# A decoder trunk on one core: the opening, GpSimd's work of the first stage and the weight of the output norm are arranged in another way

## The chip, the cores and the metric

The kernel runs as one program on one core of a Trainium2 chip. The core has TensorE (PE, with its weight loads as PEld), VectorE (DVE), ScalarE (ACT), GpSimd (POOL) and SyncE (SP, which issues DMAs), each with an instruction stream of its own; they meet by semaphores. SBUF holds the tiles, PSUM what TensorE writes. The metric is the time of one execution in microseconds (us) on the device; lower is better.

## The reference

Two layers work on 256 tokens of width 1024. Each mixes the tokens, cross-attends into 256 memory tokens, and applies an MLP. Only the first mixer is touched:

```python
z = rmsnorm(x, g) @ w_in
u, q, k, v, gate, beta_l, alpha_l = split_cols(z, A_SIZES)   # 512 x 5, 4, 4
y_pool = multiscale_pool(u, pool_w, pool_scale)
y_dn = gated_deltanet(q, k, v, gate, beta_l, alpha_l, ...)
x = x + concatenate([y_pool, y_dn]) @ w_out
```

The delta net (4 heads of 128) takes q, k and v through a short causal convolution and silu, and builds in each chunk of 64 tokens a lower triangular matrix from k k^T, beta and the decay. It solves `(I + a_low) T = I`, scans over the chunks, and ends with `rmsnorm(o, o_norm) * silu(gate)`, where `o_norm` holds one weight for each of a head's 128 channels.

## The kernel before

Every large matmul is done three times with float32 split into a high and a low part (`mm3`, L195 to L197: hi by hi, lo by hi, hi by lo). A weight tile comes by DMA on SP into one of four `raw` buffers; ScalarE makes `hi` from it (L185), VectorE, now and then GpSimd, the rest `lo` (L186). An activation that leaves PSUM is split likewise by `evac_hl` into `hh` (ScalarE, L243) and `hl` (VectorE, L247). PSUM has three pools: four `acc`, two `mb`, two `tp`.

After 13 warm-up matmuls (L145) the first mixer, `mixer0`, opens in an order written by hand for ScalarE, VectorE and TensorE. It norms x (sums of squares of token block 0 on ScalarE, `bn_stats` of block 1 on VectorE, the power -0.5 on GpSimd, L277), writes the two scales into diagonal matrices `dr` (L393), and transposes and scales x at once with real matmuls x·diag (L401). With the transposed x it computes the `a_ba` projection (beta, alpha and half of the gate) and two blocks of `a_k`. `conv_silu` does the convolution (`ct`, L416 to L421; its output `cv`, L426).

From there the order of the steps is the list `MIX`: `g1` the other half of the gate, `kn0`, `kn1` the transposes of k to tokens (L515) with their sums of squares and the copy into `pk`, `cum` the decay, `q0` to `q3`, `v0` to `v3`, `u0` to `u3` projection blocks, `kr` the norms of k (`sA`, `sK`, `sV`), `e0`, `e1` the decay matrices (`kk`, `am`, L547; mask `et`, L545), `i0`, `i1` the start of the inverse of 32x32 blocks (`ec`, the masked copies `al`, `T`, its transpose `bc`, L580 to L591), `inv1` to `inv6` its steps (L574), `mem` and `k0` to `k8` the memory tokens' norm, transposes (`memT`, L325) and keys, `pk` the scaling of `pk` (L560), `qn`, `vn`, `t1` to `t4` the scan and its outputs, `po0` to `po3` the pooling. A scheduler then places the instructions of each engine; the DMA of a weight starts when a `raw` buffer comes free. GpSimd multiplies the gate by half the output weight (`GO`, `onh`, L453).

Of the kernel before, what the change touches and what calls it, by code (L numbers as in the profile page):

```python
# [67 lines left out]
def trunk(ctx: ExitStack, tc: tile.TileContext, A, out, upto=99):  # L68
# [308 lines left out]
    def mixer0():  # L377
        hT = []
        dr = [gt('ct', 4)[:, :P] for _ in range(2)]

        def norm():

            r, s2, bn, mv = (small([P, w], f"n0_{i}", 1) for i, w in enumerate((2, 2, 12, 2)))
            for n in range(2):
                sumsq(xs[0][n], s2[:, n:n + 1])
                dve.bn_stats(bn[:, 6 * n:6 * n + 6], xs[1][n])
            dve.tensor_add(r[:, 0:1], s2[:, 0:1], s2[:, 1:2])
            rsqrt_into(r[:, 0:1], r[:, 0:1], EPS, D)
            dve.bn_aggr(mv, bn)
            dve.scalar_tensor_tensor(r[:, 1:2], mv[:, 0:1], mv[:, 0:1], mv[:, 1:2], op0=ALU.mult, op1=ALU.add)  # L390
            rsqrt_into(r[:, 1:2], r[:, 1:2], EPS, 1)
            for t in range(2):
                dve.tensor_scalar(dr[t], ident, r[:, t:t + 1], None, op0=ALU.mult)  # L393

        def tokens(n):

            ps = [tp() for _ in range(2)]
            for i in range(2):
                for j in range(2):
                    for t in range(2):  # L400
                        pe.matmul(ps[i][:, j * S + t * P:j * S + (t + 1) * P], x_block(t, 4 * n + 2 * i + j), dr[t], start=True, stop=True)  # L401
            new = [hpair() for _ in range(4)]

            for k in (0, 2, 1, 3):
                evac_hl(ps[k // 2][:, (k % 2) * S:(k % 2 + 1) * S], new[k], V("a_ln")[:, 4 * n + k:4 * n + k + 1])
            hT.extend(new)
# [42 lines left out]
        def ev_gate(t, q, ps):  # L449
            if t == 0:  # L450
                dve.tensor_scalar(onh, V("o_norm"), 0.5, None, op0=ALU.mult)
            gate_half(t, ps, S)
            pool.tensor_tensor(b3(GO[t], P), b3(GO[t], P), onh.unsqueeze(1).to_broadcast([P, 4, P]), op=ALU.mult)  # L453

        with tc.manual_schedule(engines={mybir.EngineType.Activation, mybir.EngineType.DVE, mybir.EngineType.PE}):
            norm()
            tokens(0)
            us = list(wunit("a_ba", 0, 1056))
            tokens(1)
            us += wunit("a_ba", 1, 1056)  # L460
# [944 lines left out]
```

## Time and profile before

| | us |
|---|---|
| median of 3 runs (873.1 to 874.53) | 874.26 |
| the profiled execution's own time | 871.83 |
| its span in the trace | 870.0 |
| TensorE busy | 848.6 (98%) |
| VectorE busy | 541.3 (62%) |
| ScalarE busy | 492.8 (57%) |
| GpSimd busy | 214.4 (25%) |

The profile takes one execution. Its span is the time from the first to the last recorded event. A timeline row gives start and duration in us, the engine, the line of the kernel, the operation, output<-input, the shapes and a count; in brackets how long the engine had been idle before and who released it. Windows give each engine's busy time in a stretch, with the clock that was granted to TensorE (1.00 is 2.4 GHz) and the share of the DMA engines' time.

### The profile page before, as it was taken

What the parts mean: (1) busy time and instruction counts of PE and PEld (TensorE: products, weight loads), DVE (VectorE), ACT (ScalarE), POOL (GpSimd) and SP (SyncE); (2) the same over time, 40 slices, a digit from 0 to 9 for tenths busy, and PEclk for the clock granted to TensorE, in tenths of its full rate; (3) what the DMA queues carried; (4) which work ended last, traced back from release to release, by engine and by line L of the source; (5) the groups of instructions that cost most, each with busy time, mean ns of one, the idle gap of its engine ahead of it and who ended that gap; (6) DMA issues with size and microseconds to landing.
All of it is one profiled execution on the core that took longest, in us unless ns stands there. A gap on an engine that the chain in (4) does not pass through costs nothing.

```text
span 870.0 us, 16157 instructions
## 1 busy us (share of the span) xinstructions
PE 848.6 (98%) x6247; PEld 769.0 (88%) x6247; DVE 541.3 (62%) x1050; ACT 492.8 (57%) x996; POOL 214.4 (25%) x195
## 2 busy tenths in 40 slices
PE   7889999999999999999999999999999999999996
PEld 5888999899889999999889888888998999999995
DVE  5988756656566555555557697865565755555554
ACT  5774556655565554454576767856554655544552
POOL 1142520310013222222233454544200122222220
PEclk9999999999999999999999999999999999999999
DMA  7632443666446566656654421135644466566641
GB/s 263 222 97 84 132 140 113 178 197 194 160 135 212 184 184 190 192 187 184 218 156 160 147 81 66 50 116 160 185 147 146 150 212 189 181 188 193 192 147 49
DMA packets 41261, 138.84 MB, mean 160 GB/s; under 512 B 4576, under 2 KB 5088, under 8 KB 41184
## 3 DMA queue, kind: packets, MB, share of 16 engines
q1 hardware_dynamic: 40320, 136.28, 50.2%
q10 hardware_dynamic: 864, 1.52, 0.5%
q8 instruction: 49, 0.80, 0.4%
q14 instruction: 28, 0.23, 0.1%
HBM read 136.74 MB, written 1.05 MB: 158 GB/s over the span
## 4 chain that ended last, share of the span: by engine, by line
PE 89%; DVE 4%; ACT 1%; issue 0%; POOL 0%; POOLq 0%; ACTq 0%; DVEq 0%
PE acc L197 12%; PE acc L195 12%; PE acc L196 12%; PE mb L196 10%; PE mb L195 10%; PE mb L197 10%; PE tp L195 4%; PE tp L196 4%; PE tp L197 4%; PE acc L574 1%; PE tp L257 1%; PE tp L1222 1%; DVE ct L419 1%; PE tp L1225 1%; DVE lo L186 1%; PE tp L1205 0%
## 5 line engine op out<-in xcount | busy, mean ns | idle before, releaser
L185 ACT ACTIVATE hi<-raw 128x1024 fp32r<-128x1024 f32 (+2 forms) x256 | 264.1, 1034 | 260.5 <-PE acc L197 117.5
L186 DVE TENSOR_TENSOR lo<-raw,hi 128x1024 fp32r<-128x1024 f32 (+3 forms) x227 | 277.4, 1224 | 197.6 <-ACT hi L185 196.9
L197 PE MATMUL acc<-hi,hl 128*128 128x512 f32 (+3 forms) x496 | 188.5, 380 | 0.0
L196 PE MATMUL acc<-lo,hh 128*128 128x512 f32 (+3 forms) x496 | 188.4, 380 | 0.0
L195 PE MATMUL acc<-hi,hh 128*128 128x512 f32 (+3 forms) x496 | 188.2, 379 | 0.0
L195 PE MATMUL mb<-hh,hi 128*128 128x256 f32 x640 | 182.7, 287 | 0.5 <-ACT ct L417 0.5
L196 PE MATMUL mb<-hl,hi 128*128 128x256 f32 x640 | 182.3, 286 | 0.0
L197 PE MATMUL mb<-hh,lo 128*128 128x256 f32 x640 | 180.5, 283 | 0.0
L924 POOL TENSOR_TENSOR rs<-rs 128x256 f32<-128x256 f32 x64 | 74.6, 1175 | 238.3 <-ACT rs L922 238.3
L196 PEld LDWEIGHTS mb<-hl,hi 128*128 128x128 f32 x640 | 122.0, 191 | 2.2 <-issue 1.0
L195 PEld LDWEIGHTS mb<-hh,hi 128*128 128x128 f32 x640 | 121.9, 191 | 1.9 <-ACT ct L417 0.7
L197 PEld LDWEIGHTS mb<-hh,lo 128*128 128x128 f32 x640 | 121.9, 191 | 0.0
L197 PEld LDWEIGHTS acc<-hi,hl 128*128 128x128 f32 x496 | 93.3, 188 | 17.6 <-DVE hl L245 0.3
L196 PEld LDWEIGHTS acc<-lo,hh 128*128 128x128 f32 x496 | 93.5, 188 | 17.2
L195 PEld LDWEIGHTS acc<-hi,hh 128*128 128x128 f32 x496 | 93.3, 188 | 17.3
L186 POOL TENSOR_TENSOR lo<-raw,hi 128x1024 fp32r<-128x1024 f32 (+2 forms) x29 | 68.7, 2369 | 92.6 <-ACT hi L185 85.9
L195 PE MATMUL tp<-hh,hi 128*128 128x256 f32 x256 | 72.1, 282 | 0.0
L196 PE MATMUL tp<-hl,hi 128*128 128x256 f32 x256 | 71.9, 281 | 0.0
L197 PE MATMUL tp<-hh,lo 128*128 128x256 f32 x256 | 71.7, 280 | 0.0
L197 PEld LDWEIGHTS tp<-hh,lo 128*128 128x128 f32 x256 | 48.4, 189 | 0.0
L196 PEld LDWEIGHTS tp<-hl,hi 128*128 128x128 f32 x256 | 48.2, 188 | 0.0
L195 PEld LDWEIGHTS tp<-hh,hi 128*128 128x128 f32 x256 | 48.2, 188 | 0.0
(304 smaller groups left out, 1257.5 us busy)
## 6 DMA issues: line engine op xcount, KB each, us to landing
raw<-in_ff_w_dram SPq DMA_DIRECT2D x128, 512.0 KB, 3.6
raw<-in_xa_wk_dram SPq DMA_DIRECT2D x16, 512.0 KB, 4.0
raw<-in_xa_wv_dram SPq DMA_DIRECT2D x16, 512.0 KB, 3.8
raw<-in_xa_wq_dram SPq DMA_DIRECT2D x16, 512.0 KB, 3.9
raw<-in_xa_wo_dram SPq DMA_DIRECT2D x16, 512.0 KB, 3.5
raw<-in_a_w_out_dram SPq DMA_DIRECT2D x8, 512.0 KB, 3.5
raw<-in_c_q_dram SPq DMA_DIRECT2D x8, 512.0 KB, 4.2
raw<-in_c_w_out_dram SPq DMA_DIRECT2D x8, 512.0 KB, 3.2
```

The lines of the kernel that those rows point to most:

```text
L185: act.activation(hi[:, :n], raw[:, :n], AF.Copy)
L186: lo_eng.tensor_sub(lo[:, :n], raw[:, :n], f(hi[:, :n]))
L195: pe.matmul(ps, sh, mh, start=start, stop=False)
L196: pe.matmul(ps, sh, ml, start=False, stop=False)
L197: pe.matmul(ps, sl, mh, start=False, stop=stop)
L257: pe.transpose(ps[:, j * S + t * P:j * S + (t + 1) * P], src(t, k0 + j), ident)
L419: dve.scalar_tensor_tensor(c[:, 3 - j:], xp[:, :S - 3 + j], w[:, j:j + 1], c[:, 3 - j:], op0=ALU.mult, op1=ALU.add)
L574: pe.matmul(ps[o, c], lhs[o, c], rhs[o, c], start=True, stop=True)
L924: pool.tensor_tensor(sq, rl, rl, op=ALU.mult)
L1222: pe.matmul(po[rows, :S], v, pts[a][bi][:, :S], start=bi == 0, stop=False)
L1225: pe.matmul(po[:, :S], CV[g][:64], pcT[:64], start=False, stop=True)
```

## The change

The opening scales x itself by the norm into four tiles `xn` (VectorE the first half of the columns, ScalarE the second) and transposes them with plain `pe.transpose`. The sum of squares of a token block's first half is ScalarE's, that of its second half VectorE's (`tensor_tensor_reduce`). The second halves of x are loaded on ScalarE's DMA queue; two `a_ba` tiles share a `raw` buffer. `onh` shrinks to one number for each channel and is applied as the scale when the transposed output leaves PSUM in `out_t`, where GpSimd's multiply of the gate is dropped. The first copies `ec` of the inverse, `pk_scale` and the copies to `memT` go to ScalarE, the wide mask product `al` to VectorE; the `et` masks become steps of their own late in the list, and GpSimd too now follows the list. The list has another order.

```diff
-MIX = """g1 kn0 kn1 cum q0 q1 kr e0 i0 e1 v0 q2 v1 i1 inv1 v2 q3 inv2 mem v3 inv3 vn0 inv4 k0 inv5 u0
-u1 u2 pk u3 k1 k2 qn0 pw qn1 po0 inv6 po1 vn1 po2 k3 k4 t1 k5 k6 t2 po3 t3 k7 k8 t4 sh0""".split()
+MIX = """g1 kn1 q0 kn0 cum q1 kr e1 e0 v0 i0 q2 i1 inv1 v1 v2 q3 inv2 inv3 mem v3 k0 inv4 vn0 inv5 u0 et1 u1 u2 pk u3 et0 k1 k2 pw qn0 qn1
+po0 inv6 po1 vn1 po2 k3 k4 t1 k5 k6 t2 po3 t3 k7 k8 t4 sh0""".split()
...
-    ("w2_k", P), ("w2_v", 64), ("o_norm", P),
+    ("w2_k", P), ("w2_v", 64), ("o_norm", 1),
...
+        raw = wraw.tile([P, 1056], F32, tag="raw", name=nm("raw"))
+        for j in range(2):
+            first[name, i + j] = raw[:, j * n:(j + 1) * n]
+            nc.sync.dma_start(first[name, i + j], A[name][i + j])
+    for t in range(2):
+        nc.sync.dma_start(xs[t][0], A["x"][t, 0])
+        nc.scalar.dma_start(xs[t][1], A["x"][t, 1])
+    nc.sync.dma_start(cst[:, :P], A["cst"][:, :P])
+    early("a_ba", 0, 528)
     nc.sync.dma_start(vec, A["vec"])
-    for i in range(4):
-        early("a_ba", i, 528)
+    early("a_ba", 2, 528)
     nc.sync.dma_start(cst[:, P:], A["cst"][:, P:])
...
-                dve.tensor_copy(memT[:, k0:k0 + 2, :], b3(ps, S))
+                act.activation(memT[:, k0:k0 + 2, :], b3(ps, S), AF.Copy)
...
+        hT = [None] * KT
+        xn = [[gt('cv', 6) for _ in range(2)] for _ in range(2)]
+        n_r, n_s, n_q = (small([P, 2], f"n0_{i}", 1) for i in range(3))
+        def norm_act(t):
+            act.activation(junk, xs[t][0], AF.Square, scale=D ** -0.5, accum_out=n_s[:, t:t + 1])
+        def norm_dve(t):
+            dve.tensor_tensor_reduce(out=xn[t][1], in0=xs[t][1], in1=xs[t][1], scale=1.0 / D, scalar=EPS,
+                                     op0=ALU.mult, op1=ALU.add, accum_out=n_q[:, t:t + 1])
+        def norm_pow(t):
+            r = n_r[:, t:t + 1]
+            dve.tensor_add(r, n_s[:, t:t + 1], n_q[:, t:t + 1])
+            pool.tensor_tensor(r, r, mhalf[:, :1], op=ALU.pow)
+        def norm_mul(t):
+            r = n_r[:, t:t + 1]
+            dve.tensor_scalar(xn[t][0], xs[t][0], r, None, op0=ALU.mult)
+            act.activation(xn[t][1], xs[t][1], AF.Copy, scale=r)
+        def evac_x(ps, k):
+            hT[k] = hpair()
+            evac_hl(ps[k // 2][:, (k % 2) * S:(k % 2 + 1) * S], hT[k], V("a_ln")[:, k:k + 1])
...
-        onh = gt('onh', 1, P)
+        onh = small([P, 1], "onh", 1)
...
-            if t == 0:
-                dve.tensor_scalar(onh, V("o_norm"), 0.5, None, op0=ALU.mult)
             gate_half(t, ps, S)
-            pool.tensor_tensor(b3(GO[t], P), b3(GO[t], P), onh.unsqueeze(1).to_broadcast([P, 4, P]), op=ALU.mult)
...
+            pt = [tp(), tp(), acc(), acc()]
+            def flip(t):
+                for k in range(KT):
+                    pe.transpose(pt[k // 2][:, (k % 2) * S + t * P:(k % 2) * S + (t + 1) * P], xn[t][k // 4][:, (k % 4) * P:(k % 4 + 1) * P], ident)
+            norm_act(0)
+            norm_dve(0)
+            norm_pow(0)
+            norm_act(1)
+            norm_mul(0)
+            norm_dve(1)
+            flip(0)
+            norm_pow(1)
+            us = [wsplit("a_ba", 0, 528)]
+            norm_mul(1)
+            flip(1)
+            us.append(wsplit("a_ba", 1, 528))
             ps = [acc() for _ in range(2)]
-            for j, (hi, lo) in enumerate(us):
-                h3, l3 = b3(hi[:, :528], 264), b3(lo[:, :528], 264)
-                for t in range(2):
-                    for k2 in range(2):
-                        k = 2 * j + k2
+            def first_mm(j):
+                for k2 in range(2):
+                    k = 2 * j + k2
+                    h3, l3 = (b3(z[:, :528], 264) for z in us[j])
+                    for t in range(2):
                         mm3(ps[t][:, :264], tuple(a[:, t * P:(t + 1) * P] for a in hT[k]), (h3[:, k2], l3[:, k2]), k == 0, k == KT - 1)
+            for j in range(4):
+                for k in (2 * j, 2 * j + 1):
+                    evac_x(pt, k)
+                if j < 2:
+                    us.append(wsplit("a_ba", j + 2, 528))
+                first_mm(j)
...
+        dve.tensor_scalar(onh, V("o_norm"), 0.5, None, op0=ALU.mult)
...
-            e_, et, am = gt('e', 2), gt('et', 2), gt('am', 2)
+            e_, am = gt('et', 2), gt('am', 2)
...
-            pool.tensor_tensor(b3(et, P), b3(e_, P), U.unsqueeze(1).to_broadcast([P, 4, P]), op=ALU.mult)
...
+        def e_mask(t):
+            pool.tensor_tensor(b3(AT[t], P), b3(AT[t], P), U.unsqueeze(1).to_broadcast([P, 4, P]), op=ALU.mult)
         def pk_scale():
             for t, w in ((0, ela), (1, sK)):
-                pool.tensor_tensor(b3(pk[t], P), b3(pk[t], P), w[:, t].unsqueeze(2).to_broadcast([P, 4, P]), op=ALU.mult)
+                for h in range(4):
+                    act.activation(pk[t][:, hs(h)], pk[t][:, hs(h)], AF.Copy, scale=w[:, t, h:h + 1])
...
-                (dve if t == 0 else pool).tensor_copy(b3(ec, 32)[o], b3(E[t], P)[o, :, o])
+                act.activation(b3(ec, 32)[o], b3(E[t], P)[o, :, o], AF.Copy)
             am = gt('al', 2, 5 * P)
             a4 = am.rearrange("p (l h j) -> p l h j", l=5, h=4)
             m3 = b3(C("masks"), 32)
-            for l0, l1 in ((0, 1), (1, 5)):
+            def part(l0, l1):
                 n = l1 - l0
-                (pool if l0 else dve).tensor_tensor(a4[:, l0:l1], b3(ec, 32).unsqueeze(1).to_broadcast([P, n, 4, 32]),
-                                                    m3[:, l0:l1].unsqueeze(2).to_broadcast([P, n, 4, 32]), op=ALU.mult)
+                dve.tensor_tensor(a4[:, l0:l1], b3(ec, 32).unsqueeze(1).to_broadcast([P, n, 4, 32]),
+                                  m3[:, l0:l1].unsqueeze(2).to_broadcast([P, n, 4, 32]), op=ALU.mult)
+            part(0, 1)
             T_ = gt('T', 2)
             dve.tensor_tensor(b3(T_[:, :P], 32), C("ident32").unsqueeze(1).to_broadcast([P, 4, 32]), a4[:, 0], op=ALU.subtract)
             B_ = gt('bc', 2, P)
             dve.transpose(B_, T_[:, :P])
+            part(1, 5)
...
-                evac_hl(ps[:, hs(h)], (hi[:, t * P:(t + 1) * P], lo[:, t * P:(t + 1) * P]))
+                evac_hl(ps[:, hs(h)], (hi[:, t * P:(t + 1) * P], lo[:, t * P:(t + 1) * P]), onh)
...
-        run(MIX, step)
+        with tc.manual_schedule(engines={mybir.EngineType.Pool}):
+            run(MIX, step)
...
-    put("o_norm", g["a_o_norm"][0][None])
+    put("o_norm", g["a_o_norm"][0][:, None])
```

VectorE at the opening, before: `n` are the small tiles of the norm, `onh` the output weight, `ct` the diagonal matrices.

```order
L386 BN_STATS n_2_14_135<-x_84 128x6
L386 BN_STATS n_2_14_135<-x_85 128x6
L387 TENSOR_TENSOR n_0_12_133<-n_1_13_134 128x1
L451 TENSOR_SCALAR onh_127<-vec 128x128
L276 TENSOR_SCALAR n_0_12_133<-n_0_12_133 128x1
L389 BN_AGGR n_3_15_136<-n_2_14_135 128x2
L390 SCALAR_TENSOR_TENSOR n_0_12_133<-n_3_15_136 128x1
L276 TENSOR_SCALAR n_0_12_133<-n_0_12_133 128x1
L393 TENSOR_SCALAR ct_125<-cst,n_0_12_133 128x128
L393 TENSOR_SCALAR ct_126<-cst,n_0_12_133 128x128
```

VectorE at the opening now (ISA is the multiply-and-sum and its read-out, `cv_123` to `cv_126` the scaled x, `raw_93` and `raw_97` the a_ba tiles):

```order
L389 ISA cv_124,n_2_10_129<-x_83 128x512
L389 ISA n_2_10_129 128x1
L394 TENSOR_TENSOR n_0_8_127<-n_1_9_128,n_2_10_129 128x1
L494 TENSOR_SCALAR onh_130<-vec 128x1
L399 TENSOR_SCALAR cv_123<-x_82,n_0_8_127 128x512
L389 ISA cv_126,n_2_10_129<-x_85 128x512
L389 ISA n_2_10_129 128x1
L394 TENSOR_TENSOR n_0_8_127<-n_1_9_128,n_2_10_129 128x1
L188 TENSOR_TENSOR lo_159<-raw_93,hi_158 128x528
L399 TENSOR_SCALAR cv_125<-x_84,n_0_8_127 128x512
L188 TENSOR_TENSOR lo_173<-raw_93,hi_172 128x528
L249 SCALAR_TENSOR_TENSOR hl_179<-tp_136,vec,hh_178 128x256
```

`onh`, which reads `vec`, stands before the first scaling of x, and the statistics of the second block behind it.

ScalarE at the opening now; `x_83` and `x_85` are the second halves of x:

```order
L493 ACTIVATE ea_360<-vec 128x4
L400 ACTIVATE cv_124<-x_83,n_0_8_127 128x512
L187 ACTIVATE hi_158<-raw_93 128x528
L400 ACTIVATE cv_126<-x_85,n_0_8_127 128x512
L187 ACTIVATE hi_172<-raw_93 128x528
L245 ACTIVATE hh_178<-tp_136,vec 128x256
L245 ACTIVATE hh_182<-tp_136,vec 128x256
L187 ACTIVATE hi_186<-raw_97 128x528
L245 ACTIVATE hh_202<-tp_137,vec 128x256
L245 ACTIVATE hh_206<-tp_137,vec 128x256
L187 ACTIVATE hi_210<-raw_97 128x528
L187 ACTIVATE hi_277<-raw_275 128x1024
```

`ea`, which reads `vec`, stands ahead of the scaling; all hi of a_ba and the first of a_k stand ahead of the last four `hh`, which follow after two more a_k tiles.

VectorE at the start of the inverse, before:

```order
L186 TENSOR_TENSOR lo_973<-raw_970,hi_972 128x1024
L547 SCALAR_TENSOR_TENSOR am_675<-acc_668,sA_464,e_673 128x128 x4
L547 SCALAR_TENSOR_TENSOR am_710<-acc_703,sA_464,e_708 128x128
L580 COPY ec_686<-am_675 32x128 x4
L547 SCALAR_TENSOR_TENSOR am_710<-acc_703,sA_464,e_708 128x128
L586 TENSOR_TENSOR al_691<-ec_686,cst 128x128
L547 SCALAR_TENSOR_TENSOR am_710<-acc_703,sA_464,e_708 128x128
L589 TENSOR_TENSOR T_694<-cst,al_691 128x128
L547 SCALAR_TENSOR_TENSOR am_710<-acc_703,sA_464,e_708 128x128
L591 STREAM_TRANSPOSE bc_696<-T_694 128x128
```

VectorE there now (the e matrix of the second block comes first):

```order
L561 SCALAR_TENSOR_TENSOR am_693<-acc_687,sA_463,et_692 128x128 x4
L417 SCALAR_TENSOR_TENSOR ct_734<-ct_734,vec 128x254
L417 SCALAR_TENSOR_TENSOR ct_786<-ct_786,vec 128x255
L417 SCALAR_TENSOR_TENSOR ct_734<-ct_734,vec 128x253
L605 TENSOR_TENSOR al_748<-ec_743,cst 128x128
L605 TENSOR_TENSOR al_748<-ec_743,cst 128x512
L609 TENSOR_TENSOR T_750<-cst,al_748 128x128
L424 SCALAR_TENSOR_TENSOR cv_741<-ct_734 128x256
L611 STREAM_TRANSPOSE bc_752<-T_750 128x128
L417 SCALAR_TENSOR_TENSOR ct_786<-ct_786,vec 128x254
L605 TENSOR_TENSOR al_800<-ec_795,cst 128x128
L417 SCALAR_TENSOR_TENSOR ct_786<-ct_786,vec 128x253
```

The `ec` copies are gone from VectorE, and both wide `al` masks (128x512) stand in it.

ScalarE there now:

```order
L559 ACTIVATE et_692<-et_692 128x512
L414 ACTIVATE ct_786<-mb_761 128x256
L415 ACTIVATE ct_786<-mb_761,vec 128x256
L273 ACTIVATE junk,ss_1167<-mem_1162 128x512
L187 ACTIVATE hi_1434<-raw_1432 128x1024
L598 ACTIVATE ec_743<-am_693 32x128 x4
L414 ACTIVATE ct_916<-mb_891 128x256
L415 ACTIVATE ct_916<-mb_891,vec 128x256
L419 ACTIVATE ct_734<-ct_734 128x256
L598 ACTIVATE ec_795<-am_672 32x128 x4
L187 ACTIVATE hi_1477<-raw_1475 128x1024
```

The two groups of four `ec` copies stand behind a `hi` and the convolutions' copies of two blocks. Between the matmuls of `kk` and the first of `inv1`, TensorE has 90 projection matmuls now and had 72.

## Rows read from the trace of the kernel before

**Rows 1.** The page: busy time, share and instructions of each engine.
```profile
PE 848.6 (98%) x6247; PEld 769.0 (88%) x6247; DVE 541.3 (62%) x1050; ACT 492.8 (57%) x996; POOL 214.4 (25%) x195
```

**Rows 2.** TensorE's waits: line, releaser: us in total, times, longest.
```profile
PE tp L401 <- DVE ct L393: 3.4, 1, 3.4
...
PE acc L574 <- DVE bc L591: 2.6, 1, 2.6
...
PE acc L574 <- DVE rstd L285: 0.9, 1, 0.9
```

**Rows 3.** Windows: from:to, length, busy PE, PEld, DVE, ACT, POOL, clock, DMA, GB/s.
```profile
5.50:9.00 3.50, 0.14 (x2) 0.06 (x1) 1.73 (x8) 0.93 (x3) 0.98 (x2) 1.00 1.04 388
...
40.00:70.00 30.00, 24.75 (x210) 24.33 (x209) 26.66 (x51) 19.30 (x53) 16.39 (x14) 0.89 0.37 116
45.00:50.00 5.00, 5.00 (x33) 5.00 (x31) 2.28 (x4) 3.79 (x17) 0.00 (x0) 0.66 0.65 202
50.00:60.00 10.00, 10.00 (x88) 10.00 (x88) 9.44 (x25) 9.91 (x26) 6.24 (x5) 1.00 0.16 39
...
70.00:90.00 20.00, 19.09 (x461) 17.55 (x460) 16.71 (x43) 10.47 (x26) 2.35 (x2) 1.00 0.27 82
```

**Rows 4.** Timeline of the opening, to the first a_k evacuation.
```profile
6.92 0.69 DVE L386 BATCH_NORM_STATS2 n<-x 128x6 f32<-128x512 f32 x1 [2.08 <-DMA x<-in_x_dram]
7.55 0.20 ACT L479 ACTIVATE ea<-vec 128x4 f32<-128x4 f32 x1 [0.54 <-DMA vec<-in_vec_dram]
8.02 1.08 POOL L277 TENSOR_TENSOR n<-n,mhalf 128x1 f32<-128x1 f32 x2 [6.27 <-DVE n L389]
8.95 2.35 PE L401 MATMUL tp<-ct,x 128*128 128x128 f32 x16 [3.36 <-DVE ct L393]
...
11.33 0.84 ACT L243 ACTIVATE hh<-tp,vec 128x256 fp32r<-128x256 f32 x2 [0.42 <-PE tp L401]
12.73 1.17 ACT L185 ACTIVATE hi<-raw 128x528 fp32r<-128x528 f32 x2
17.68 1.06 ACT L185 ACTIVATE hi<-raw 128x1024 fp32r<-128x1024 f32 x1 [0.23 <-DMA raw<-in_a_k_dram]
...
26.95 0.39 PE L195 MATMUL mb<-hh,hi 128*128 128x256 f32 x1 [0.51 <-ACT ct L417]
```

**Rows 5.** Timeline from 36 to 70 us, around the two stalls.
```profile
36.00 1.22 DVE L186 TENSOR_TENSOR lo<-raw,hi 128x1024 fp32r<-128x1024 f32 x1
...
40.15 3.50 POOL L453 TENSOR_TENSOR GO<-GO,onh 128x512 f32<-128x512 f32 x2 [31.00 <-DVE GO L443]
40.32 2.21 DVE L186 TENSOR_TENSOR lo<-raw,hi 128x1024 fp32r<-128x1024 f32 x1
42.45 1.48 DVE L426 SCALAR_TENSOR_TENSOR cv<-ct 128x256 f32<-128x256 f32 x1
43.98 0.44 PE L515 MATMUL tp<-cst,cv 128*128 128x128 f32 x2 [2.66 <-DVE cv L426]
...
55.56 1.26 DVE L527 TENSOR_TENSOR sK<-sA,egc 128x8 f32<-128x8 f32 x1
59.17 2.95 DVE L580 COPY ec<-am 32x128 f32<-32x128 f32 x4
62.42 1.20 DVE L586 TENSOR_TENSOR al<-ec,cst 128x128 f32<-128x128 f32 x1
64.70 0.87 PE L574 MATMUL acc<-bc,al 32*32 32x32 f32 x32 [2.60 <-DVE bc L591]
68.79 0.28 DVE L586 TENSOR_TENSOR al<-ec,cst 128x128 f32<-128x128 f32 x1
```

**Rows 6.** Groups by form, 0 to 130 us: count, busy, mean ns, idle before.
```profile
L621 ACT ACTIVATE B<-bc 32x128 f32<-32x128 f32 x4 | 1.2, 307 | 1.1 <-DVE bc L606 1.1
...
L545 POOL TENSOR_TENSOR et<-e,cst 128x512 f32<-128x512 f32 x2 | 2.7, 1337 | 1.1 <-ACT e L544 1.1
...
L325 DVE COPY memT<-tp 128x512 f32<-128x512 f32 x4 | 2.6, 676 | 0.5 <-PE tp L324 0.5
```

More of the change, by code (lines that the diff above doesn't have):

```diff
@@ L125, in early @@
     def early(name, i, n):
-        first[name, i] = wraw.tile([P, 1040], F32, tag="raw", name=nm("raw"))
-        nc.sync.dma_start(first[name, i][:, :n], A[name][i])
-    for n in range(2):
-        for t in range(2):
-            nc.sync.dma_start(xs[t][n], A["x"][t, n])
-        if n == 0:
-            nc.sync.dma_start(cst[:, :P], A["cst"][:, :P])
+        raw = wraw.tile([P, 1056], F32, tag="raw", name=nm("raw"))
[7 more added lines that the diff above has]
+    early("a_ba", 0, 528)
     nc.sync.dma_start(vec, A["vec"])
-    for i in range(4):
-        early("a_ba", i, 528)
+    early("a_ba", 2, 528)
     nc.sync.dma_start(cst[:, P:], A["cst"][:, P:])
@@ L163, in wload @@
             return first[name, i]
-        raw = wraw.tile([P, 1040], F32, tag="raw", name=nm("raw"))
+        raw = wraw.tile([P, 1056], F32, tag="raw", name=nm("raw"))
         nc.sync.dma_start(raw[:, :n], A[name][i])
@@ L377, in mixer0 @@
     def mixer0():
[L378 to L406, printed above, removed]
+        hT = [None] * KT
[17 more added lines that the diff above has]
+            evac_hl(ps[k // 2][:, (k % 2) * S:(k % 2 + 1) * S], hT[k], V("a_ln")[:, k:k + 1])
         conv = {}
@@ L449, in ev_gate @@
         def ev_gate(t, q, ps):
-            if t == 0:
-                dve.tensor_scalar(onh, V("o_norm"), 0.5, None, op0=ALU.mult)
             gate_half(t, ps, S)
-            pool.tensor_tensor(b3(GO[t], P), b3(GO[t], P), onh.unsqueeze(1).to_broadcast([P, 4, P]), op=ALU.mult)
         with tc.manual_schedule(engines={mybir.EngineType.Activation, mybir.EngineType.DVE, mybir.EngineType.PE}):
[L456 to L460, printed above, removed]
-            ps = [acc() for _ in range(2)]
-            for j, (hi, lo) in enumerate(us):
-                h3, l3 = b3(hi[:, :528], 264), b3(lo[:, :528], 264)
-                for t in range(2):
-                    for k2 in range(2):
-                        k = 2 * j + k2
-                        mm3(ps[t][:, :264], tuple(a[:, t * P:(t + 1) * P] for a in hT[k]), (h3[:, k2], l3[:, k2]), k == 0, k == KT - 1)
+            pt = [tp(), tp(), acc(), acc()]
[14 more added lines that the diff above has]
+            us.append(wsplit("a_ba", 1, 528))
+            ps = [acc() for _ in range(2)]
+            def first_mm(j):
[3 more added lines that the diff above has]
+                    for t in range(2):
+                        mm3(ps[t][:, :264], tuple(a[:, t * P:(t + 1) * P] for a in hT[k]), (h3[:, k2], l3[:, k2]), k == 0, k == KT - 1)
+            for j in range(4):
[4 more added lines that the diff above has]
+                first_mm(j)
         for t in range(2):
@@ L507, in cum @@
             act.activation(egc, gc, AF.Exp)
-        pk = []
+        pk = [None] * 2
         def k_nat(t):
@@ L519, in k_nat @@
             dve.tensor_copy(kn, ps)
-            pk.append(kn)
+            pk[t] = kn
         def k_norm():
@@ L528, in k_norm @@
             dve.scalar_tensor_tensor(sV, rk, 0.5, beta, op0=ALU.mult, op1=ALU.mult)
-        E, AT, qe = [], [], []
+        E, AT, qe = [None] * 2, [None] * 2, []
         def e_mat(t):
@@ L554, in e_mat @@
                 act.activation(qe[0], bc, AF.Exp)
-            E.append(am)
-            AT.append(et)
+            E[t] = am
+            AT[t] = e_
+        def e_mask(t):
+            pool.tensor_tensor(b3(AT[t], P), b3(AT[t], P), U.unsqueeze(1).to_broadcast([P, 4, P]), op=ALU.mult)
         def pk_scale():
             for t, w in ((0, ela), (1, sK)):
-                pool.tensor_tensor(b3(pk[t], P), b3(pk[t], P), w[:, t].unsqueeze(2).to_broadcast([P, 4, P]), op=ALU.mult)
+                for h in range(4):
+                    act.activation(pk[t][:, hs(h)], pk[t][:, hs(h)], AF.Copy, scale=w[:, t, h:h + 1])
         def heads(ps, lhs, rhs):
@@ L799, in mixer0 @@
             step.update((f"{s}{i}", f_) for i, f_ in enumerate(fs))
-        for s, f_ in (("kn", k_nat), ("e", e_mat), ("i", inv0), ("qn", q_nat), ("vn", v_nat)):
+        for s, f_ in (("kn", k_nat), ("e", e_mat), ("et", e_mask), ("i", inv0), ("qn", q_nat), ("vn", v_nat)):
             step.update((f"{s}{t}", lambda t=t, f_=f_: f_(t)) for t in range(2))
-        run(MIX, step)
+        with tc.manual_schedule(engines={mybir.EngineType.Pool}):
+            run(MIX, step)
         last = lambda: out_t(1, late["y1"])
```

## Prediction

> **What bounds the kernel now.** I read the busy shares first, then what TensorE waited for, then the stretches of those waits in the windows and the timeline. TensorE is busy in 848.6 us of 870.0 [rows 1], so all that can be won is what it waits plus what it loses at a low clock. The list of its waits [rows 2] has four entries in the first 66 us that the change touches: 3.4 us before the first x block, 2.6 and 0.9 before the 32x32 inverse, and 2.7 before the k transposes (that one stands with its start in [rows 5]). With 0.5 before a k block [rows 4] they sum to 10.1. The windows add the clock: in 40 to 70 it was granted 0.89 on average, and 0.66 in 45 to 50, which is 1.7 us at the lower level (1.2 GHz) after the first stall; 0.11 x 30 = 3.3 says that the second stall had the same dip [rows 3]. From 50 to 60, 88 matmuls took 10.0 us, so one of 256 columns costs 0.11 to 0.12 when nothing is late (I count 0.12).
>
> Why were the operands late? From 40.15 on GpSimd multiplied the gate by the output weight (two of 1.75 us). Beside it VectorE's subtraction took 2.21 instead of 1.22, and the `cv` behind it 1.48, where an evacuation of as many elements takes 0.42; the k transposes waited for that `cv` [rows 4, 5]. Before the inverse the same is seen beside GpSimd's mask and pk work: `sK` 1.26 us for 8 elements, the four `ec` copies 2.95, `al` 1.20 where its twin at 68.79 took 0.28 [rows 5]. I read this as VectorE and GpSimd slowing each other; the trace shows it in every such pair, but never VectorE with GpSimd taken away.
>
> **The opening.** In [rows 4] `vec` lands at 7.55, since ScalarE's `ea` starts then behind its DMA. By the order, the changed kernel has `onh` and `ea`, which read `vec`, ahead of the scaling of x on both engines: the first transposes can't start before `vec`, which now has two units of a_ba ahead of it. The bytes up to and with it were 4 x 256 + 64 + 238 = 1326 KB, and become 4 x 256 + 64 + 528 + 175 = 1791 (the ACT queue's x halves included). At the 388 GB/s of 5.5 to 9 [rows 3] that is 1.2 us later, 8.75, if the queues share alike, and 7.55 if `vec` isn't held up at all; I take 8.3, nearer to the late end, as the DMA engines stood at 100% there. From it: the pass over x, the statistics of its second half and the small operations on VectorE, two such passes at 0.69 and 0.3 between them, and one `pow` of 0.54, make 2.2. Then ScalarE scales x (0.6), and does hi, two `hh`, hi, two `hh`, hi and the first a_k hi: 0.6 + 3 x 0.59 + 4 x 0.42 + 1.06 = 5.1 [rows 4]. VectorE follows with three a_k subtractions of 1.22 and one `hl` (0.4, as an `hh`): 4.1. TensorE has 45 matmuls left behind that `hl`, 5.4 us. So a_ba and the first a_k blocks end at 8.3 + 16.8 = 25.1, where before they ended at 26.95 - 0.51 = 26.4. **Gain 1.3, and the 0.5 behind it goes, since a_k is loaded earlier: 1.8** (from -0.2 with a lower clock, below, to 2.9 with an early `vec`). The plain transposes themselves, 16 for 32 records of 0.14, are covered by the waiting on both sides and count nothing in this sum; were they not, they save up to 2.
>
> **The first stall.** The two multiplies on GpSimd are gone; the weight now rides as the scale of an evacuation that was there before (16 instructions, as many as before, so nothing). The subtraction and `cv` give back 1.0 + 1.0 of the 2.7, and k_nat(1) now comes first with the q block between the two; what is left of the wait I put at 0.3. With the dip that followed it, **2.7 + 1.7 - 0.3 = 4.1**.
>
> **The inverse.** TensorE asked at 64.70 - 2.60 = 62.1 after 72 matmuls behind `kk`, so it finished `kk` at 53.5 and `bc` came 11.2 us later [rows 5]. Now 90 matmuls stand there, 10.7 us. Of the 11.2, `ec` falls from 2.95 to 4 x 0.31 on ScalarE (nearest row: its `B` copies of the same shape [rows 6]), `al` by 0.9, `sK` by 1.0: 7.6, if no engine is late. If so the wait of 2.6, the 0.9 and the dip of 1.6 go: **5.1**.
>
> **What is late next.** The stretch of 30 us would lose 2.7 + 2.6 + 0.9 + 3.3 = 9.5. ScalarE idled 30 - 19.3 = 10.7 in it [rows 3], so 1.2 stay, against eight `ec` copies for 2.5: it is short by **1.3**. VectorE worked 26.66; the slowed pieces give back 1.0 + 1.0 + 1.0 + 0.9, `ec` 2.95, and the two 128x512 masks come over from GpSimd for 0.68 each (the memT copy of that size [rows 6]): 20.2 of 20.5, with no room, so I let one subtraction be late, **1.2**. In 70 to 90 ScalarE idled 9.5 and gets four memT copies (2.7) and eight pk scalings (2.5 by the `B` row; 1.2 if they cost half): room enough, but a transposed memory block waits for its PSUM buffer, one copy, **0.7**. Bounds of these three: 0, and all the 7.7 that ScalarE gets (a rival). GpSimd is the other end: the et masks (1.34 each) now stand in its fixed order among the pooling windows; nothing but VectorE's attention multiply waits for them, with two memory-key blocks to hide them. In 70 to 90 GpSimd does 2.35 of 20 [rows 3, 6]. I take 0, at most 2.7.
>
> Sum: 1.8 + 4.1 + 5.1 - 3.2 = **7.8**. Span 870.0 to 862.2, the profiled run's own 871.83 to 864.0; that run is 2.4 under the median of 874.26, from which I count: **866.5**.
>
> **The clock in the opening.** Before the first stall's dip TensorE had stood still for 2.66 us and went on with transposes, two at 43.98 and more behind the blocks [rows 5]; the granted clock was down from 45. In the opening it stood still for 3.4 us and went on with real matmuls against a diagonal, and the clock stayed at 1.00 [rows 2, 3, 4]. Now the opening too goes on with transposes. The Trainium skill ("TensorE: Matmul & The Clock Gate", Part 4: PE-mode transpose) says that transpose mode doesn't count as TensorE work in the way matmuls do, so the full clock isn't reached by it. By that rule the opening's first matmuls would run at the lower level and the sum would be 6.4; without it, 7.8. The trace agrees for the stall at 43.98; that it shows no transposes after the pause in the opening leaves it open.
>
> **Rivals.**
> 1. *The clock falls in the opening.* For it: the pair of pauses above. Against it: four pauses are few, and the 2.66 one may have dipped for another reason. The dip costs 1.7 by [rows 3], of which some 0.3 lies in TensorE's wait for the evacuations: 874.26 - 6.4 = **867.9**.
> 2. *The inverse stalls again.* `ec`, ScalarE's, stands behind hi and conv work of its own, and VectorE has no room. The stall comes back with its dip: 2.6 + 1.6 for the 1.3 that I book, 2.9 worse: **869.4**. For it: ScalarE short by 1.3; against: 18 more matmuls before the inverse.
> 3. *VectorE isn't slowed by GpSimd.* Then both stalls stay and the opening remains less 0.7: 874.26 - 1.1 = **873.2**. Against it: the twin `al`, 1.20 and 0.28.
> 4. *ScalarE becomes the bound; slower.* It gets 7.7 us (ec 2.5, pk 2.5, memT 2.7). If TensorE waits for all of it, and for the clock twice again (3.3), that is 11.0 against 1.8 + 4.1: 5.1 slower, **879.4**. It turns slower once more than 2.6 of the 7.7 land on TensorE with both dips. Against it: 10.7 + 9.5 of idle ScalarE.
>
> **How the numbers follow.** Forecast 0.45, rival 1 0.25, rival 2 0.18, rival 3 0.05, rival 4 0.07. About 0.2% (1.75 us) is what a measurement of this kernel tells from no change. The first three are faster, 0.88, less 0.02 for their own spread; rival 3 and that spread make 0.06; slower 0.08. Low end: no new waits and an early `vec` gain 12.1, 862.2, and the runs shown lie up to 1.2 under their median: 861. High end: rivals 1 and 2 together give 870.8; with the transposes also a little late, 872.
>
> **What would show it.** Opening: transposes start 2.2 + 0.5 us behind `vec`; a granted clock of 1.00 up to 20 us (0.66 is rival 1). First stall: no `cv` over 0.5 and no wait at the k transposes over 0.5. Inverse: `al` near 0.28, `ec` near 0.31, a wait under 1.5, the clock at 1.00 in 40 to 70. GpSimd's masks late with nobody waiting. I am wrong if VectorE's pieces stay slow without GpSimd, if a wait of over 2 us stands at another step of the first 130 us, or if the time after the first stage moves by over 1 us.

## The result, and the profile after

The changed kernel took 863.76 us (median of 4 runs, 863.62 to 865.69) against 873.68 of before (871.96 to 874.53): ratio 0.9894, 95% interval 0.9873 to 0.9915, so 9 to 10 us faster. A second measurement gave 0.9884 (0.9865 to 0.9903). The forecast was 866.5, the range 861 to 872. The profiled execution is the slowest of the four, 865.69 with a span of 863.9.

TensorE's waits after (line, releaser: us in total, times, longest), to be read beside [rows 2]:

```profile
PE tp L455 <- DVE cv L399: 4.6, 2, 3.2
PE acc L592 <- DVE bc L611: 1.2, 1, 1.2
...
PE mb L197 <- ACT hi L187: 0.6, 2, 0.4
```

The wait of 2.7 before the k transposes is gone, that before the inverse fell from 2.6 + 0.9 to 1.2, and the opening waits 4.6 at its transposes.

Windows after, with the columns of [rows 3]:

```profile
5.50:9.00 3.50, 0.31 (x3) 0.17 (x3) 1.03 (x6) 1.52 (x5) 0.55 (x1) 1.00 1.03 365
...
11.05:14.45 3.40, 3.16 (x15) 3.16 (x16) 2.01 (x5) 2.70 (x6) 0.00 (x0) 0.50 0.64 221
...
45.00:50.00 5.00, 5.00 (x47) 5.00 (x46) 4.35 (x10) 4.84 (x20) 0.00 (x0) 1.00 0.83 274
...
62.30:65.60 3.30, 3.30 (x26) 3.08 (x25) 2.90 (x7) 2.70 (x7) 0.00 (x0) 0.50 0.00 0
```

The dip behind the k transposes is gone (45 to 50: 47 matmuls at 1.00, before 33 at 0.66). One stands in the opening now, and a short one at the inverse.

The opening and the two places of [rows 4, 5] in the timeline after:

```profile
8.20 0.20 ACT L493 ACTIVATE ea<-vec 128x4 f32<-128x4 f32 x1 [1.69 <-DMA vec<-in_vec_dram]
8.20 0.15 DVE L494 TENSOR_SCALAR onh<-vec 128x1 f32<-128x1 f32 x1 [2.36 <-DMA vec<-in_vec_dram]
...
8.83 0.66 PE L455 MATMUL tp<-cst,cv 128*128 128x128 f32 x4 [3.19 <-DVE cv L399]
...
13.18 0.47 ACT L245 ACTIVATE hh<-tp,vec 128x256 fp32r<-128x256 f32 x1 [0.68 <-DVE hl L249]
...
15.35 0.48 ACT L245 ACTIVATE hh<-tp,vec 128x256 fp32r<-128x256 f32 x1 [0.81 <-DVE hl L249]
...
20.76 0.48 DVE L249 SCALAR_TENSOR_TENSOR hl<-acc,vec,hh 128x256 fp32r<-128x256 f32 x1
...
26.84 0.28 PE L197 MATMUL acc<-hi,hh 128*128 128x256 f32 x1
...
41.73 1.22 DVE L188 TENSOR_TENSOR lo<-raw,hi 128x1024 fp32r<-128x1024 f32 x1
43.03 0.48 DVE L417 SCALAR_TENSOR_TENSOR ct<-ct,vec 128x255 f32<-128x255 f32 x1
...
57.85 1.27 ACT L598 ACTIVATE ec<-am 32x128 f32<-32x128 f32 x4
...
59.15 0.90 DVE L605 TENSOR_TENSOR al<-ec,cst 128x128 f32<-128x128 f32 x2 [0.15 <-ACT ec L598]
...
60.69 0.30 DVE L611 STREAM_TRANSPOSE bc<-T 128x128 f32<-128x128 f32 x1
...
61.14 0.87 PE L592 MATMUL acc<-bc,al 32*32 32x32 f32 x32 [1.22 <-DVE bc L611]
```

`vec` lands at 8.20 and the transposes start 0.63 behind it. VectorE's pieces have their usual lengths (the subtraction 1.22, not 2.21), the `ec` copies 0.32 each. But the a_k blocks end no earlier: TensorE goes on behind them at 26.84, and before it was free at 26.95 - 0.51 = 26.44. The 0.51 of waiting behind them is gone, which leaves 0.1.

How far TensorE is ahead is read where both kernels have done the same matmuls: at the last one of the gate before the k transposes, at the first one behind them and their projection blocks, and at ScalarE's first sum of squares behind the mixer. In each pair the first row is before, the second after:

```profile
38.37 0.29 PE L197 MATMUL acc<-hi,hl 128*128 128x256 f32 x1
38.27 0.29 PE L199 MATMUL acc<-hi,hl 128*128 128x256 f32 x1
...
49.45 0.38 PE L535 MATMUL acc<-cst,ld 128*128 128x128 f32 x2
45.13 0.38 PE L550 MATMUL acc<-cst,ld 128*128 128x128 f32 x2
...
160.33 0.63 ACT L271 ACTIVATE junk<-x 128x512 bf16<-128x512 f32 x1 [0.48 <-DVE x L305]
154.20 0.63 ACT L273 ACTIVATE junk<-x 128x512 bf16<-128x512 f32 x1 [0.16 <-DVE x L307]
```

The lead is 0.1, then 4.3, then 6.1, and it is 6.1 at the end of the two spans. In the profile of experiment 9, the same kernel without the dip at the inverse, it is 0.2, 4.4, 7.8 and 7.7.

### The profile page after: what moved, and what is told of

Read it like the earlier page. It is cut to its first block, busy times and chain, and to the rows that moved or that the text cites. A ratio compares the mean times of both kernels' runs of the same rounds, so it can differ in the third digit from the quotient of the medians.

```text
span 863.9 us, 16134 instructions
## 1 busy us (share of the span) xinstructions
PE 847.2 (98%) x6231; PEld 766.0 (89%) x6231; DVE 534.3 (62%) x1043; ACT 500.9 (58%) x1018; POOL 202.9 (23%) x185
## 4 chain that ended last, share of the span: by engine, by line
PE 89%; DVE 4%; ACT 3%; issue 1%; DMA 1%; SPq 0%; POOL 0%; POOLq 0%; DVEq 0%; ACTq 0%
PE acc L197 12%; PE acc L199 12%; PE acc L198 12%; PE mb L197 10%; PE mb L198 10%; PE mb L199 10%; PE tp L197 4%; PE tp L198 4%; PE tp L199 4%; PE acc L592 1%; PE tp L259 1%; PE tp L1244 1%; DVE lo L188 1%; ACT hi L187 1%; ACT junk L273 1%
```

## The experiments

Each was timed beside the kernel before, which itself had 873.5 beside 1 to 4, 875.3 beside 5 to 8 (another chip) and 874.3 beside 9 to 12. So the ratios are compared; 0.001 is 0.87 us. Where a cost is given with two bounds, it is counted from the changed kernel's two ratios.

**1. GpSimd's gate multiply put back** into the changed kernel; the other engines' order is the same.

```diff
             gate_half(t, ps, S)
+            pool.tensor_tensor(b3(GO[t], P), b3(GO[t], P), one.unsqueeze(1).to_broadcast([P, 4, P]), op=ALU.mult)
```

> The changed kernel with GpSimd's two 128x512 multiplies of the gate put back (by a tile of ones, right behind the gate as in the kernel before); every other engine's order is unchanged, and nothing waits for the product before the end of the stage. Theory 1 (GpSimd's work slows VectorE beside it): near 40 us one subtraction takes about 2.2 us instead of 1.2 and a cv or ct 1.0 to 1.5 instead of 0.4; of these 2 us 1 to 2 reach TensorE, with a clock dip of 1.7 if it stands still over 2 us: 1 to 4 us slower than the changed kernel. Rival (the new order of the steps removed the first stall): VectorE's rows as in the changed kernel or slowed without a wait, time within 0.5 us.

865.42 us, ratio 0.9911 (0.9894 to 0.9928): 1.5 us slower than 863.9. GpSimd, VectorE and TensorE in its timeline:

```profile
41.73 3.51 POOL L451 TENSOR_TENSOR GO<-GO,one 128x512 f32<-128x512 f32 x2 [30.93 <-DVE GO L443]
41.84 2.26 DVE L188 TENSOR_TENSOR lo<-raw,hi 128x1024 fp32r<-128x1024 f32 x1
44.02 1.51 DVE L417 SCALAR_TENSOR_TENSOR ct<-ct,vec 128x255 f32<-128x255 f32 x1
...
48.85 0.61 PE L523 MATMUL tp<-ld,cst 128*128 128x4 f32 x4 [1.67 <-DVE pk L537]
```

The same two instructions take 2.26 and 1.51 beside GpSimd, 1.22 and 0.48 without. Theory 1 holds. TensorE waits 1.67, now at the transposes of the decay, and in this execution (867.01, the slowest of the six) the clock was at 0.50 from 50.7 to 54.1.

**2. The kernel before without that multiply.**

```diff
-            pool.tensor_tensor(b3(GO[t], P), b3(GO[t], P), onh.unsqueeze(1).to_broadcast([P, 4, P]), op=ALU.mult)
...
-                evac_hl(ps[:, hs(h)], (hi[:, t * P:(t + 1) * P], lo[:, t * P:(t + 1) * P]))
+                evac_hl(ps[:, hs(h)], (hi[:, t * P:(t + 1) * P], lo[:, t * P:(t + 1) * P]), onh)
```

> The kernel before, with nothing but the gate's multiply on GpSimd left out and the output weight applied as the scale when the transposed output leaves PSUM. Theory 1: the subtraction at 40 us takes 1.2 and the cv 0.4, the wait before the k transposes falls from 2.7 to about 0.7 and the dip behind it goes: 3.0 to 4.1 us faster than before, the inverse's stall unchanged. Rival (order): the wait stays over 2 us and the time within 1 us of before.

871.73 us, ratio 0.9977 (0.9963 to 0.9992): 2.0 us faster than before (0.7 to 3.2), where I had put 3 to 4.1. VectorE is at its usual speed, but the wait stays at 1.8:

```profile
41.91 1.06 ACT L185 ACTIVATE hi<-raw 128x1024 fp32r<-128x1024 f32 x1 [2.62 <-DMA raw<-in_a_q_dram]
42.87 0.64 ACT L442 ACTIVATE ct<-acc 128x256 f32<-128x256 f32 x2
...
45.07 0.42 DVE L426 SCALAR_TENSOR_TENSOR cv<-ct 128x256 f32<-128x256 f32 x1
...
45.55 0.44 PE L514 MATMUL tp<-cst,cv 128*128 128x128 f32 x2 [1.81 <-DVE cv L426]
```

ScalarE stood before a `hi` of a_q whose DMA was late, and the gate and the last `cv` queued behind it. In the profile of before no late DMA stood there:

```profile
38.29 1.06 ACT L185 ACTIVATE hi<-raw 128x1024 fp32r<-128x1024 f32 x1 [1.42 <-PE acc L197]
39.25 0.64 ACT L442 ACTIVATE ct<-acc 128x256 f32<-128x256 f32 x2
```

So this wait has a cause of its own. Experiment 6 has it too, with the old opening and the new order of the steps, and 8, with the new opening and the old order, has none: it goes with the opening, in executions whose clock fell there (2 and 6), and not with the order.

**3. vec loaded before the a_ba tiles** (in the changed kernel).

```diff
-    early("a_ba", 0, 528)
     nc.sync.dma_start(vec, A["vec"])
+    early("a_ba", 0, 528)
```

> The changed kernel with the DMA of vec ahead of the first two a_ba tiles. If vec is what holds the first transposes: vec lands 0.7 to 1.3 us earlier (528 KB less ahead of it), the transposes start as much earlier, and the a_k blocks end 0.3 to 1.2 earlier: 0.3 to 1.2 us faster than the changed kernel. Rival (the a_ba tiles or the a_k tiles set the pace of the opening): transposes earlier, time within 0.3 us.

863.50 us (863.04 to 863.59), ratio 0.9882 (0.9866 to 0.9899). `vec` landed at 6.80 instead of 8.20, of which 0.5 was left at the end of the a_k blocks and some 0.4 at the end. It is the fastest version measured, by less than the intervals tell apart.

**4. 27 warm-up matmuls in place of 13.**

```diff
-WARM = 13
+WARM = 27
```

> The changed kernel with 27 warm-up matmuls in place of 13, so that TensorE stands still before the first transposes for well under 1 us instead of 3.2. If the pause lowered the clock in the opening: granted 1.00 from 9 to 20 us, 1 to 1.4 us faster than the changed kernel. Rival (transposes don't hold the clock up, whatever stands before them): 0.5 again in a stretch between 9 and 15 us, time within 0.4 us.

864.14 us, ratio 0.9890 (0.9872 to 0.9907): no gain. The clock did stay up, in two windows of this run, the second with the transposes:

```profile
4.70:8.80 4.10, 4.10 (x20) 1.66 (x17) 1.44 (x6) 1.93 (x6) 0.55 (x1) 1.00 1.05 390
8.80:15.00 6.20, 4.52 (x31) 3.58 (x30) 4.26 (x10) 3.76 (x8) 0.99 (x1) 1.00 0.77 277
```

Its a_k blocks end at 26.86, as with the dip (26.84). So the dip in the opening cost nothing; experiment 5 shows what sets the end. What lowers the clock there isn't shown: this run has both a shorter pause and more matmuls before it, and the profile of before has 1.00 from 4.1 to 45.1, over a pause of 3.36 [rows 4].

**5. Neighbouring x blocks in different PSUM tiles.**

```diff
-            evac_hl(ps[k // 2][:, (k % 2) * S:(k % 2 + 1) * S], hT[k], V("a_ln")[:, k:k + 1])
+            evac_hl(ps[k % 4][:, (k // 4) * S:(k // 4 + 1) * S], hT[k], V("a_ln")[:, k:k + 1])
...
-                    pe.transpose(pt[k // 2][:, (k % 2) * S + t * P:(k % 2) * S + (t + 1) * P], xn[t][k // 4][:, (k % 4) * P:(k % 4 + 1) * P], ident)
+                    pe.transpose(pt[k % 4][:, (k // 4) * S + t * P:(k // 4) * S + (t + 1) * P], xn[t][k // 4][:, (k % 4) * P:(k % 4 + 1) * P], ident)
```

> The changed kernel with the transposed x blocks spread so that neighbouring blocks lie in different PSUM tiles (block k in tile k mod 4 instead of k div 2). Theory (the opening's chain ScalarE-VectorE sets its end, and each second hh waits for the hl of the block beside it in its tile, 0.7 and 0.8 us, twice): these waits go, the last a_k matmul ends 1.0 to 1.6 us earlier, the kernel is 0.7 to 1.6 us faster than the changed one. Rival (TensorE's own work or the weights' DMA set the end of the opening): hh waits gone, end of the a_k blocks and the time within 0.3 us.

865.49 us, ratio 0.9893 (0.9869 to 0.9917). The waits of `hh` for `hl` went and the a_k blocks ended at 26.10, 0.74 earlier: that chain was a bound, with 0.74 for the 1.5 of waits that went. But the scheduler now put 74 matmuls ahead of inv1 instead of 90, and the runs fell in two groups, three at 863.6 to 864.1 (mean granted clock 0.994 to 0.996) and three at 866.9 to 867.7 (0.991). No gain.

**6. The opening of before** (loads, norm, matmuls against diagonals) in the changed kernel.

```diff
-            pt = [tp(), tp(), acc(), acc()]
...
+            norm()
+            tokens(0)
+            us = list(wunit("a_ba", 0, 1056))
```

> The changed kernel with the opening of the kernel before (loads, norm, scaling matmuls, order of the first evacuations); all else as changed. By the prediction's term the opening gives 1.8: 1.8 us slower than the changed kernel. By the trace, in which the a_k blocks end 0.1 us earlier and the gate 0.5 us: 0.1 to 0.7 us slower. Rival (the opening costs as its clock falls): the same or faster.

867.80 us, ratio 0.9919 (0.9897 to 0.9942): 2.2 to 3.1 us slower than the changed kernel (by its two ratios). Here the clock fell in the old opening (0.50 from 9.85 to 13.20):

```profile
9.10 3.73 PE L401 MATMUL tp<-ct,x 128*128 128x128 f32 x16 [2.39 <-DVE ct L393]
...
28.32 0.39 PE L195 MATMUL mb<-hh,hi 128*128 128x256 f32 x1 [0.32 <-ACT ct L417]
```

The first sixteen records take 3.73 where [rows 4] have 2.35, and TensorE comes to the block behind the a_k blocks 1.4 us later than there (28.32 for 26.95). Experiment 2, with the same opening and a low clock from 10.2 to 17.0, comes there at 29.46. The new opening comes there at 26.84, 26.74 and 26.86 with dips of 3.4, 6.8 and 0 us (the changed kernel, experiments 9 and 4).

That is half of the cost. The other half is the wait of experiment 2, which came back with the old opening although the steps have the new order:

```profile
PE tp L513 <- DVE cv L426: 1.4, 1, 1.4
```

```profile
40.49 1.06 ACT L185 ACTIVATE hi<-raw 128x1024 fp32r<-128x1024 f32 x1 [2.29 <-DMA raw<-in_a_q_dram]
41.46 0.64 ACT L442 ACTIVATE ct<-acc 128x256 f32<-128x256 f32 x2
```

The scheduler put 77 matmuls ahead of inv1 here instead of 90; the wait there was 0.9, and the clock stayed at 1.00 through the inverse.

**7. The start of the inverse on the engines of before.**

```diff
-                act.activation(b3(ec, 32)[o], b3(E[t], P)[o, :, o], AF.Copy)
+                (dve if t == 0 else pool).tensor_copy(b3(ec, 32)[o], b3(E[t], P)[o, :, o])
...
+                (pool if l0 else dve).tensor_tensor(a4[:, l0:l1], b3(ec, 32).unsqueeze(1).to_broadcast([P, n, 4, 32]),
+                                                    m3[:, l0:l1].unsqueeze(2).to_broadcast([P, n, 4, 32]), op=ALU.mult)
```

> The changed kernel with the start of the inverse on the engines of before (ec copies on VectorE for token block 0 and GpSimd for 1, wide al masks on GpSimd). Theory 1 (GpSimd's work beside VectorE slows it and its own pieces are long): ec 0.7 instead of 0.31 each, bc later by 1.5 to 3 us, TensorE's wait before inv1 2.5 to 4 instead of 1.2 and a dip behind it: 1.5 to 4 us slower than the changed kernel. Rival (the 18 more matmuls ahead of inv1 removed the stall, the engines don't matter): within 0.5 us.

876.57 us, ratio 0.9986 (0.9960 to 1.0012): 8.0 to 8.9 us slower, twice the most that I had expected. Its wait and two stretches:

```profile
PE acc L592 <- DVE bc L609: 3.6, 1, 3.6
```

```profile
60.00:65.00 5.00, 1.37 (x27) 1.20 (x26) 5.00 (x10) 2.22 (x7) 3.48 (x6) 0.81 0.00 0
...
63.20:93.80 30.60, 29.46 (x452) 27.47 (x453) 16.68 (x42) 10.14 (x26) 3.03 (x4) 0.50 0.19 54
```

`bc` is late by the old way, and the clock then stays at 0.50 for 30.6 us, through most of the inverse (its last 32x32 matmul starts at 103.5). Of 12 runs 7 have a mean clock of 0.976 to 0.980 and 876.5 to 878.3 us, 5 one of 0.989 to 0.992 and 868.8 to 870.6. Even these are some 5 us slower than the changed kernel.

**8. The steps in the order of before.**

```diff
-MIX = """g1 kn1 q0 kn0 cum q1 kr e1 e0 v0 i0 q2 i1 inv1 v1 v2 q3 inv2 inv3 mem v3 k0 inv4 vn0 inv5 u0 et1 u1 u2 pk u3 et0 k1 k2 pw qn0 qn1
+MIX = """g1 kn0 kn1 cum q0 q1 kr e0 et0 i0 e1 et1 v0 q2 v1 i1 inv1 v2 q3 inv2 mem v3 inv3 vn0 inv4 k0 inv5 u0
...
```

> The changed kernel with the steps in the order of before (et masks right behind their e steps, as GpSimd had them). If the order of the list carries the gain: a wait of 1 to 2 us before the k transposes as in the kernel before without its multiply (1.8), and one before inv1 of 1 to 3, 2 to 5 us slower than the changed kernel. Rival (the engines carry it): within 1 us.

871.25 us, ratio 0.9957 (0.9940 to 0.9974): 5.5 to 6.4 us slower. The k transposes don't wait, with the old order and the new opening; TensorE waits 2.3 before the inverse, and the clock falls there and again in its later steps:

```profile
PE acc L592 <- DVE bc L611: 2.3, 1, 2.3
```

```profile
85.00:97.00 12.00, 12.00 (x189) 11.20 (x185) 8.02 (x18) 6.01 (x18) 1.68 (x6) 0.57 0.20 53
```

**9. The changed kernel again**, on the chip of 10 to 12.

> The changed kernel once more, beside the three others on the same chip: 9 to 10 us faster than the kernel before, as measured first, and the row against which the other three are read. If its times fall in two groups like those of the kernel with the banks apart (863.7 and 867), the clock after a wait at the inverse is what differs between them.

863.90 us (863.62 to 864.08), ratio 0.9884 (0.9865 to 0.9903): one group. In its profile the same wait of 1.2 stands before inv1, with the clock at 1.00:

```profile
60.00:65.00 5.00, 3.98 (x107) 3.83 (x108) 4.70 (x13) 4.94 (x14) 0.00 (x0) 1.00 0.02 3
```

**10. Experiment 7 with inv1 listed behind q3.**

```diff
-MIX = """g1 kn1 q0 kn0 cum q1 kr e1 e0 v0 i0 q2 i1 inv1 v1 v2 q3 inv2 inv3 mem v3 k0 inv4 vn0 inv5 u0 et1 u1 u2 pk u3 et0 k1 k2 pw qn0 qn1
+MIX = """g1 kn1 q0 kn0 cum q1 kr e1 e0 v0 i0 q2 i1 v1 v2 q3 inv1 inv2 inv3 mem v3 k0 inv4 vn0 inv5 u0 et1 u1 u2 pk u3 et0 k1 k2 pw qn0 qn1
```

> The kernel with the inverse's start on the engines of before, with inv1 listed behind q3: 120 matmuls of 256 columns stand ahead of it in place of 96, 2.9 us more; fewer are left between the later steps of the inverse. Theory (the 3.6 us wait lets the clock fall, and in the inverse's small matmuls it stays low for up to 31 us, which is 5 to 12 us): wait under 1, the clock at 1.00 from 60 to 95 us or a stretch of under 7 us at 0.5, time 866 to 870. Rival (the old engines cost by themselves all along the inverse): 873 to 877 as without the cover.

874.35 us, ratio 1.0004 (0.9992 to 1.0015). The wait of 3.6 fell to 0.9 and some shorter ones, and the clock fell all the same:

```profile
67.20:91.00 23.80, 22.98 (x395) 20.96 (x396) 12.61 (x31) 7.94 (x21) 2.54 (x3) 0.50 0.29 87
```

My theory that the one long wait makes the low clock falls. I suspected a thinned inverse, with less projection work among its small matmuls, but the runs don't show it: from the first to the last 32x32 matmul there are 94 matmuls of 256 columns in the changed kernel, 85 in 7 and 57 in 10, but 79 in 6, whose clock stayed at 1.00.

**11 and 12. vec first and inv1 behind v2; in 12 also the blocks of experiment 5.**

> The changed kernel with vec loaded first and inv1 listed behind v2 (96 matmuls ahead of it for 90). Expected if the opening's 0.5 and the wait of 1.2 before inv1 are both still to be had: wait 0.5 there, 0.5 to 1.2 us faster than the changed kernel. Rival (what is won there is waited for later in the inverse, whose steps have fewer matmuls between them): within 0.3 us.

> vec first, neighbouring x blocks in different PSUM tiles, and inv1 behind v2. The opening's end 1.2 us earlier than in the changed kernel (0.5 and 0.7 by the two apart), 96 matmuls ahead of inv1. Expected if these add: 1.0 to 2 us faster than the changed kernel. Rival (ScalarE and VectorE are as late at the inverse as before, so the earlier opening turns into a longer wait there): within 0.5 us, or slower by 2 to 4 in executions whose clock falls there.

866.71 us, ratio 0.9914 (0.9890 to 0.9938), and 867.43 us, 0.9924 (0.9905 to 0.9943): 2.6 and 3.5 us slower than the changed kernel. 12 ends its a_k blocks at 25.28, 1.56 earlier, and loses it all: waits of 0.9 at the inverse, and mean clocks of 0.990 to 0.991 in five runs and 0.974 in one (880.13). In 11 four runs have 0.987 to 0.993 and 865.7 to 869.2 us, and two have 0.997 and 863.9 to 864.3: even where the clock stayed up, nothing was won.

## Why the prediction was right, and where not

- **The first stall: right, 4.1 forecast, 4.2 measured** (the lead of TensorE grows from 0.1 to 4.3 over the k transposes, in the two profiles). That GpSimd slows VectorE is shown by 1 and 2, with the work put in and taken out. What the stall is worth is less than that beside the old opening: 2 gained 2.0, as another wait of 1.8, ScalarE behind the late DMA of a_q, stood there then. The new opening takes that one away (6 has it, 8 hasn't), which the prediction counted nowhere.
- **The inverse: right in kind.** The wait went from 3.5 to 1.2, for which I had booked 1.3, and the dip is there in one of two profiles; in that execution rival 2 came by half. `ec` 0.31, `al` wide 0.68 came as read; the pk scalings cost 0.39 for 0.31, memT 0.60 for 0.68. From the k transposes to the end I had 5.1 - 3.2 = 1.9, and the two profiles have 1.8 with the dip and 3.3 without. One sum in it is off: VectorE's pieces add up to 21.2 and not 20.2 of 20.5, which makes it short, as I had assumed anyway.
- **The opening: `vec` right (8.2 for 8.3), the chain behind it 1.6 too short**: the first `hl` of the second half ended 13.0 behind `vec` for 11.4. I had missed that an `hh` waits for the `hl` of the block beside it in the same PSUM tile (0.68 and 0.81; experiment 5 takes it away and gains 0.74; the rest isn't placed). The first transposes start 0.63 behind `vec` and those of the second token block 3.1, for the one start at 2.7 that I gave as a sign. Beside an opening that keeps its clock the new one gains 0.1 to 0.2 by the time of the k transposes, where I had 1.8. By 6 it is worth 2.2 to 3.1: the old one's matmuls are on the path and lengthen with a low clock (1.4), the new one's transposes are covered, and the wait behind the DMA of a_q is gone with it (1.4).
- **Rival 1 came true and cost nothing.** The clock fell in the opening (0.50 from 11.05 to 14.45), but 4 shows the same end without it. The Trainium skill's rule ("TensorE: Matmul & The Clock Gate", Part 4: PE-mode transpose), that transposes don't count as work to the clock in the same way, didn't decide: in 4 the clock stayed at 1.00 over the transposes, and in 2 and 6 it fell over real matmuls. The dip after the first stall of before, which I took as agreeing with it, was no clear case either: behind the two transposes at 43.98 TensorE did 31 projection matmuls, to 49.3, and the clock was down from 45.1 to 48.5.
- **Rivals 3 and 4** didn't come: VectorE was fast, and ScalarE's 7.3 us of new work lay mostly in its idle time. GpSimd's late masks (the second at 106.9) made nobody wait. The time after the first stage didn't move: the lead at 160 us is the lead at the end.
- **The term that was mis-sized is the step from the profile to the median.** I took the dips of before from one profile (871.83), and added the 2.4 that the median of before lies above it to the changed kernel too: 864.0 became 866.5. The changed kernel has no such 2.4: it has 863.6 to 864.1 in experiment 9. From the profile of before to that is 7.9, nearly the sum forecast; the other 2 are what the typical execution of before takes beyond its profile. There is luck in that 7.8 met 7.7 in the profiles: the opening was put 1.6 too high, and what comes behind the k transposes 1.4 too low. That the 2 us are low clock is likely and not shown: of the 20 runs of before beside 5 to 8 the one at a mean clock of 0.995 took 871.67, five at 0.991 took 874.3 to 875.3, and three at 0.986 took 876.8 to 878.3; but three at 0.995 beside 9 to 12 spread from 871.1 to 873.5. The mean also counts low stretches that cost nothing, such as the changed kernel's opening. And no slower execution of before was profiled; in 2, at 0.990, the clock was low for 6.8 us at the opening and again at the inverse, where the profile of before has 0 and 3.4.

Open: what in the inverse lets the clock fall for 24 to 31 us in 7 and 10, for 3.4 in the profile of before, and not at all in 6 and 9. The parts put back singly cost 1.5, 2.2 to 3.1, 5.5 to 6.4 and 8.0 to 8.9 (experiments 1, 6, 8 and 7), more than the whole gain, so they aren't terms of a sum. Behind the wait at the inverse the clock was at 0.50 for 30.6 us in 7 and, in two stretches, for 13.6 in 8, which is much of their cost; in 1 it was low for 3.4 us ahead of the inverse, and in 6 not at all from there on.

## What to carry to other kernels

When an engine's instructions take twice their usual time, look which other engine works beside them, and move that work to where nobody waits. What a late operand costs before a stretch of small matmuls can be less the wait than the clock behind it (in 7 a wait of 3.6, then 30.6 us at 0.50); to shorten that one wait didn't bring the clock back (10), so look at the whole stretch. Where times of one kernel spread, list each run's mean clock before taking one profile for the typical execution, and don't carry the distance between profile and median over to the other kernel.
